# Hybrid decoder step: gates last in the input projection, weights split two products ahead, half of the first rotary keys gathered early

## The chip, the cores and the metric

One core of one Trainium2 chip runs the whole program in one launch. The metric is device microseconds of one execution, from its start to the end of the slowest (here the only) core. Engines are named as in the profile: PE (TensorE matmul), PEld (its weight load), DVE (VectorE), ACT (ScalarE), POOL (GpSimd), SP (the queue from which nearly all DMAs are issued).

## The reference, cut to what matters

Two layers of a decoder run on 1024 prompt tokens and 8 sample tokens together (1032 columns). In each layer the normalised input goes through one input projection whose columns feed three mixers:

```python
proj = h @ lp['w_in']
z, xbc, dt_raw, cq, ckv, kpe, u = jnp.split(proj, offs, axis=-1)
ssd_out, hT, conv_new = ssd_mixer(z, xbc, dt_raw, ...)   # conv width 4 + SiLU on xbc, scan, y * silu(z), norm
...                                                      # latent attention from cq, ckv, kpe
pool_out, pool_new = pool_mixer(u, pool_buf, pos, ...)   # trailing windows 2, 4, 8, 16
mix = jnp.concatenate([ssd_out, mla_out, pool_out], axis=-1) @ lp['w_out']
```

The gates z are needed only at the end of the SSD mixer (y times silu(z)); xbc after its convolution and SiLU is needed at its first chunk. The sample tokens attend over 8192 cached positions each, in pages; the rotary part of the cached keys is gathered by a page table.

## The kernel before

Activations lie transposed: 128 channels on the partitions, 1032 tokens in the free dimension. The input projection is 16 products of 128 output channels. In storage order they are: 0 the latent, 1 dt and the rotary key, 2 and 3 the query latent, 4 and 5 the pooling input u, 6 to 12 the convolved channels (6 to 8 x, 9 and 10 B, 11 and 12 C), 13 to 15 the gates z. The order in which they are computed is ORD.

A product is split in three in precision (a high and a low half of weights and of input, three matmuls for each of 8 contraction blocks) and in three thirds of tokens, so it is 72 matmuls of up to 348 columns. PSUM has four "d" banks and three "g" banks; a product takes two d and one g, so PE can be one product ahead of the evacuation.

For each product the weights take one DMA (`load_w`, line 123, tile wr), a cast of the high half on ACT (line 88, tile wh) and a subtraction for the low half on POOL (line 89, tile wl). `in_proj` loads and splits the weights of the next product before the gemm of this one. Then `evac` multiplies by the norm on DVE (line 285) and adds the bias on ACT (line 290). Products 6 to 12 are convolved on DVE (`conv`, lines 358 to 369: one long scale and three long multiply-adds, and four short ones for the sample tokens), which needs a second buffer, and two small stores per product go out on SP (lines 350 and 372), after the evacuation. Products 13 to 15 get their SiLU in `evac`, on ACT, followed by one of 8 columns for the sample tokens.

Beside the products, from index 8 on, `build` advances a side chain by one piece per product: `mla_prep` (index 8), `smp_prep` (9), `softplus` (10), `pool` (11 to 15). They are long on DVE and short on PE. The pooling piece loads spb, and the store o_spool (line 392) waits for it.

All of this shares one set of 24 buffers of 1032 columns ("a": weights, raw weights, projections, convolutions, temporaries) and one of 20 wider buffers ("b"). The 18 b buffers that hold the split input are released as the last product reads them; mv (the keys' map) takes the 19th, and the page tiles (pg), split pages (lt) and gathered rotary keys (kp) share what is left.

After the loop `conv_silu` runs SiLU over products 6 to 12 on ACT, with a function table loaded before and after, and the weave starts: `sample` (pages of all 8 sample tokens), the SSD chain and later the attention, interleaved by yields. `sample` asks for four pages, then issues 16 gathers from POOL (line 1094), eight to a kp tile, then splits the first page: high half on ACT (line 1141), low half on POOL (line 1142). `smp_kpe` multiplies the gathered keys in four blocks of four gathers each (line 1105). The SSD chain starts with decay masks (line 511 on PE, exponentials on ACT), B times C (line 544), transposes (line 558) whose results ACT and DVE copy out (lines 560 and 562), and the masked product (line 574).

Every engine takes its queue in order. The order in a queue follows the place in the program, but an instruction whose operands and buffer are there may be placed ahead of earlier ones that lack theirs; the table loads and the SiLUs of `conv_silu` are kept behind all ACT work written before them.

Of the kernel before, what the change touches and what calls it, by code (L numbers as in the profile page):

```python
# [48 lines left out]
class Net:  # L49
# [228 lines left out]
    def evac(self, o, ps, r, func=None):  # L278

        nc = self.nc  # L280
        n = T - 2 * TH
        b = self.S([128, 9], "sb", bufs=3)
        for t in range(3):
            a = slice(TH * t, min(TH * t + TH, T))
            nc.vector.tensor_tensor(out=o[:, a], in0=ps[t][:, :a.stop - a.start], in1=r[:, a], op=ALU.mult)
        nc.vector.tensor_copy(b, ps[2][:, n:n + 9])
        nc.vector.tensor_tensor(out=o[:, TP:], in0=o[:, TP:], in1=b[:, 1:9], op=ALU.add)
        if func is None:
            return b
        nc.scalar.activation(out=o[:, :TP], in_=o[:, :TP], func=func, bias=b[:, 0:1])  # L290
        if func == AF.Silu:
            nc.scalar.activation(out=o[:, TP:], in_=o[:, TP:], func=func)

    def sums(self, parts, mix=False):

# [8 lines left out]
    def in_proj(self, l, X, r):  # L304
        nc, A = self.nc, self.A
        out = self.pj = {}
        raws = {} if l else {2: self.w2}
        W = {}

        def prefetch(m):  # L310
            if m < 16 and m not in raws:
                raws[m] = self.load_w(A["win"][l, ORD[m]], 1024)

        def conv(m):
            if m < 16:
                W[m] = self.split_w(raws.pop(m), 1024)
        W[0] = self.w0
        pss = {}

        def wk(i):  # L320
            return lambda k: tuple(w[:, 128 * k:128 * k + 128] for w in W[i])
        if l == 0:

            W[1] = self.w1
            for i in range(2):
                pss[i] = self.psum3(TH)
            for ks in (range(0, 4), range(4, 8)):
                for i in range(2):
                    self.gemm(pss[i], wk(i), X, ks)
        for i, m in enumerate(ORD):  # L330
            if l or i:
                prefetch(i + 1)
                prefetch(i + WPI)
                conv(i + 1)
            if i in pss:
                ps = pss.pop(i)
            else:
                ps = self.psum3(TH)
                self.gemm(ps, wk(i), X)
            del W[i]  # L340
            t = self.C(name=f"pj{m}")
            self.evac(t, ps, r, AF.Silu if m >= 13 else AF.Identity)
            out[m] = t
            if 6 <= m < 13:
                out[m] = self.conv(l, m - 6, t)
            yield
# [26 lines left out]
        return y  # L373

    def conv_silu(self):
        for m in range(6, 13):
            y = self.pj[m]
            self.tc.keep_in_program_order(self.nc.scalar.activation(out=y, in_=y, func=AF.Silu))

# [873 lines left out]
    def sample(self, l):  # L1253
        self.held = False
        nc = self.nc
        n = NB * 4
        pages, kp, lts = {}, {}, []
        kts = {b: [] for b in range(NB + 1)}

        def want(t):  # L1260
            if t < 4 * n:
                pages[t] = self.fetch(l, t // 16, t % 16)

        def cut(t):
            if t < 4 * n:
                lts.append(self.smp_split(pages[t]))
        for i in range(FA):
            want(i)
        for i in range(16):
            self.smp_gather(l, 0, i, kts[0])  # L1270
        self.weave.spawn(self.smp_kpe(0, kts[0], kp), W_0)
        for i in range(SA):
            cut(i)
        yield W_9
        for gi in range(n):
            b, g = divmod(gi, 4)
            if g == 0:
                o = 390 * (b % 2)
                h = self.mv[:, o:o + 6]
                nc.vector.tensor_copy(h, self.qabs[:, b, :])  # L1280
                nc.vector.tensor_tensor(out=self.mv[:, 396 + o:402 + o], in0=self.qabs[:, b, :], in1=h.bitcast(F32),
                                        op=ALU.subtract)
                if b % 2 == 0:
                    og2 = self.B(name="og")[:, 0:1032].rearrange("p (b a x) -> p b a x", b=2, a=4)
                og = og2[:, b % 2]
            ss, sc = self.S([128, GP, 6], "ss", bufs=2), self.S([128, GP, 6], "scr", bufs=2)
            late = []
            for k in range(GP):
                t, c = divmod(GP * gi + k, 4)
                if c == 0:  # L1290
                    want(t + FA)
                    cut(t + SA)
                    lt = lts.pop(0)
                if b + 1 < NB:
                    e = GP * g + k
                    if e >= GS and (e - GS) % GE == 0 and (e - GS) // GE < 16:
                        self.smp_gather(l, b + 1, (e - GS) // GE, kts[b + 1])
                    if e == min(KE, 63):
                        self.weave.spawn(self.smp_kpe(b + 1, kts[b + 1], kp), max(0, KE - 63))
                if k % 2 == 0:  # L1300
                    sq = self.C(name="sqk")[:, 0:768].rearrange("p (a x) -> p a x", a=2)
                self.smp_page(b, lt, 128 * c, sq[:, k % 2, :], sc[:, k, :])
                if k % 2:
                    if len(late) == LD:
                        o, x = late.pop(0)
                        nc.vector.tensor_reduce(out=o, in_=x, axis=AX.X, op=ALU.add)  # L1306
                        del x
                    late.append((ss[:, k - 1:k + 1, :], sq.rearrange("p a (h e) -> p a h e", h=6)))
                    del sq
                yield  # L1310
            self.weave.spawn(self.smp_soft(l, gi, late, ss, sc, kp, og, pages))
# [396 lines left out]
def build(nc, tc, A):  # L1708
    with tc.tile_pool(name="c", bufs=1) as cp, tc.tile_pool(name="s", bufs=1) as sm, \
# [54 lines left out]
        for l in range(L):  # L1764
            mod = mods[l]
            if l:
                n.ahead(A["win"][l, ORD[0]])
            mid = [lambda i=i: n.ada(0, mod, i) for i in range(2)] if l == 0 else ()
            X, r = n.norm(l, xs, mod, 0, 1, V_GN1, mid)
            if l:  # L1770
                for k in range(8):
                    nc.sync.dma_start(A["xmid"][k], xs[k])
            del xs
            n.sconv = n.S([128, 7, 3, NB], "sconv", bufs=1)
            nc.sync.dma_start(n.sconv, A["sconv"][l])
            pr = n.in_proj(l, X, r)
            side = seq(n.mla_prep(l), n.smp_prep(l), n.softplus(l), n.pool(l))
            for m in range(16):
                next(pr)
                if l == 0 and 4 + m < ADB[0][0][1]:  # L1780
                    n.ada(l, mod, 4 + m)
                if m == 6:
                    n.table()
                if m >= 8:
                    next(side, None)
            for _ in side:
                pass
            del X, r, pr
            n.conv_silu()
            n.table()  # L1790
            n.weave = Weave()
            n.wqk = {}
            n.weave.spawn(n.sample(l))
            n.weave.spawn(seq(n.ssd_prompt(l), n.ssd_sample(l), n.ssd_finish(l), n.mla_prompt(l)))
            n.weave.spawn(seq(*[n.ada_blocks(a, mods[a], range(b, c), W_C) for a, b, c in ADB[l]]), W_E)
            n.weave.run()
            n.weave = None
            side = [None]
            op = n.out_proj(l, mod, (lambda m: A["xT"][m]) if l == 0 else (lambda m: A["xmid"][m]), side)
            X = {}  # L1800
            next(op)
            n.pj = None
            gs = n.norm_gain(l, mod, 4, V_GN2)
            n.up_first(l)
            side[0] = n.norm_half(0, mod, gs, 3, X)
            next(op)
            for _ in side[0]:
                pass
            for j in range(WA0):
                n.up_conv(l, WAH + j)  # L1810
            side = n.norm_half(1, mod, gs, 3, X)
            for _ in range(SD1):
                next(side)

            def sink(m, x):
                if l == L - 1:
                    nc.sync.dma_start(A["o_y"][m], x)
            xs = n.ffn(l, X, mod, side, sink)
            del X
# [1 line left out]

NA, NBUF = 24, 20
HALF = (slice(0, 512), slice(512, 1024))
ORD = (0, 1, 2, 3, 13, 14, 15, 4, 5, 6, 7, 8, 9, 10, 11, 12)

HOOK = None
W_D, W_X, W_Y, W_H = 2, 1, 1, 3
# [6 lines left out]
WAH = 3  # L1834
WPT, WPL, XPT, XPL, GUP = (0, 1, 2, 3), (0, 2, 4, 6), (), (1, 5, 7), 0
NG0, SD0, SD1, SDN, WLD = 2, 10, 6, 1, 3
WPI, GS, W_9 = 1, 16, 14
DCA, CVA = (0,), ()
SDO = 2
LD = 1  # L1840
# [169 lines left out]
```

## Time and profile before

| | us |
|---|---|
| median of 3 runs | 3703.59 (3699.99 to 3705.51) |
| profiled execution, its own time | 3702.83 |
| span of that execution in the trace | 3701.1 |
| PE busy | 3457.9 (93%) |
| DVE, ACT, POOL busy | 2346.1, 1733.8, 1542.7 |
| input projection of layer 0, evacuations | 73 to 280 |
| input projection of layer 1, evacuations | 1893 to 2113 |

PE is busy nearly all the time, so time is to be had where PE stands still or runs at the lower of its two clocks. Each layer has one input projection, and the two look alike in the trace; times below are from layer 1 unless layer 0 is named. In a timeline row the first number is the start, the second the length, and the bracket at the end says how long the engine stood idle before it and what it waited for.

### The profile page before, as it was taken

The page shows a single profiled execution, that of the slowest core. Times are in us where ns is not written, and L with a number is a line of the kernel's source. Part 1 is how long each engine was busy: PE and PEld are TensorE (multiplying, and loading weights), DVE is VectorE, ACT ScalarE, POOL GpSimd, SP SyncE. Part 2 cuts the span into 40 slices and gives each one's busy share as a digit, 9 for nine tenths or more (in the row PEclk, how much of TensorE's full clock was granted, in tenths as well). Part 3 has the DMA queues.
Part 4 walks back from the last instruction along what each step waited for, and adds up shares of the span by engine and source line. Part 5 has one row for each costly group of instructions (what it writes and reads, how often), then busy time and mean ns, then how long its engine had stood idle before and what let it go on. Part 6 is the DMA issues. An engine that isn't in the chain of part 4 may idle for free. (4 is left out here: it accounts for less than half of the span.)

```text
span 3701.1 us, 66621 instructions
## 1 busy us (share of the span) xinstructions
PE 3457.9 (93%) x23740; PEld 3103.2 (84%) x23740; DVE 2346.1 (63%) x4308; ACT 1733.8 (47%) x4459; POOL 1542.7 (42%) x1173
## 2 busy tenths in 40 slices
PE   8988999898987999999999799999988979999999
PEld 5986767677887999999999666677777979999999
DVE  4377787778778655542344687777787685555333
ACT  4216576677844333331132265677776443333220
POOL 1125454444244555542221355444452445555431
PEclk9989899999988999999999999999999989999999
DMA  5124555544443222242221346554443522121431
GB/s 197 49 57 139 167 178 159 177 144 115 141 137 98 84 83 75 80 171 88 80 81 44 84 132 185 183 147 120 117 117 117 160 83 87 70 86 69 176 99 69
DMA packets 255322, 430.10 MB, mean 116 GB/s; under 512 B 38736, under 2 KB 180944, under 8 KB 254992
## 3 DMA queue, kind: packets, MB, share of 16 engines
q1 hardware_dynamic: 246800, 409.04, 35.1%
q0 software_dynamic: 8192, 16.79, 1.8%
q8 instruction: 190, 3.11, 0.4%
q14 instruction: 140, 1.15, 0.1%
HBM read 372.84 MB, written 52.87 MB: 115 GB/s over the span
## 5 line engine op out<-in xcount | busy, mean ns | idle before, releaser
L1159 ACT ACTIVATE sqk<-psd 128x384 f32<-128x384 f32 x1024 | 496.8, 503 | 226.2 <-PE psd L135 172.7
L1142 POOL TENSOR_TENSOR lt<-pg,lt 128x512 fp32r<-128x512 f32 x256 | 310.1, 1220 | 537.7 <-ACT lt L1141 438.4
L1306 DVE TENSOR_REDUCE ss<-sqk 128x12 f32<-128x768 f32 x448 | 421.8, 945 | 131.0 <-ACT sqk L1159 129.7
L133 PE MATMUL psd<-mv,lt 128*128 128x390 f32 x1024 | 435.8, 427 | 3.3 <-ACT scr L1160 3.3
L134 PE MATMUL psd<-X,wp 128*128 128x258 f32 x1408 | 400.5, 284 | 3.2 <-DVE wp L89 3.2
L135 PE MATMUL psd<-X,wp 128*128 128x258 f32 x1408 | 400.8, 285 | 0.0
L133 PE MATMUL psd<-X,wp 128*128 128x258 f32 x1408 | 400.6, 284 | 0.0
L134 PE MATMUL psd<-mv,lt 128*128 128x390 f32 x1024 | 366.5, 358 | 6.2 <-POOL lt L1142 6.2
L135 PE MATMUL psd<-mv,lt 128*128 128x390 f32 x1024 | 366.0, 357 | 0.0
L134 PE MATMUL psg<-X,wp 128*128 128x258 f32 x1056 | 303.3, 287 | 35.5 <-DVE wp L89 35.5
L1094 POOL DMA_INDIRECT kp<-kpeT,kidx x256 | 251.7, 983 | 122.2 <-issue 93.3
L135 PE MATMUL psg<-X,wp 128*128 128x258 f32 x1056 | 302.6, 287 | 0.0
L133 PE MATMUL psg<-X,wp 128*128 128x258 f32 x1056 | 301.8, 286 | 0.0
L89 POOL TENSOR_TENSOR wl<-wr,wh 128x1024 fp32r<-128x1024 f32 x47 | 116.5, 2480 | 433.8 <-ACT wh L88 376.6
L133 PEld LDWEIGHTS psd<-mv,lt 128*128 128x128 f32 x1024 | 202.0, 197 | 97.5 <-issue 47.9
L133 PE MATMUL psd<-op,wh 128*128 128x348 f32 (+1 forms) x792 | 255.9, 325 | 18.8 <-ACT wh L88 15.9
L134 PE MATMUL psd<-op,wl 128*128 128x348 f32 (+1 forms) x792 | 254.9, 322 | 19.4 <-POOL wl L89 12.5
L134 PEld LDWEIGHTS psd<-X,wp 128*128 128x128 f32 x1408 | 268.6, 191 | 3.5 <-DVE wp L89 3.5
L133 PEld LDWEIGHTS psd<-X,wp 128*128 128x128 f32 x1408 | 269.3, 191 | 0.0
L135 PEld LDWEIGHTS psd<-X,wp 128*128 128x128 f32 x1408 | 268.9, 191 | 0.0
L135 PE MATMUL psd<-op,wh 128*128 128x348 f32 (+1 forms) x792 | 253.2, 321 | 1.8 <-POOL op L89 1.4
L89 POOL TENSOR_TENSOR wp<-wr,wp 128x512 fp32r<-128x512 f32 x128 | 166.9, 1304 | 197.9 <-ACT wp L88 195.6
(467 smaller groups left out, 9928.1 us busy)
## 6 DMA issues: line engine op xcount, KB each, us to landing
pg<-pages SPq DMA_DIRECT2D x1024, 129.0 KB
wa<-wada SPq DMA_DIRECT2D x96, 512.0 KB
wr<-wff SPq DMA_DIRECT2D x96, 512.0 KB
ar<-actd SPq DMA_DIRECT2D x44, 516.0 KB
actd<-G SPq DMA_DIRECT2D x40, 516.0 KB
wd<-wdn SPq DMA_DIRECT2D x48, 384.0 KB
wr<-win SPq DMA_DIRECT2D x32, 512.0 KB
wr<-wout SPq DMA_DIRECT2D x32, 512.0 KB
```

The costliest lines, as they stand in the source:

```text
L89: (eng or nc.gpsimd).tensor_tensor(out=l, in0=x, in1=h.bitcast(F32), op=ALU.subtract)
L133: nc.tensor.matmul(ps, wh, xh, start=start, stop=False)
L134: nc.tensor.matmul(ps, wl, xh, start=False, stop=False)
L135: nc.tensor.matmul(ps, wh, xl, start=False, stop=stop)
L1094: self.nc.gpsimd.indirect_dma_start(out=kts[-1][:, 128 * g:128 * g + 128], out_offset=None, in_=self.A["kpeT"], in_offset=bass.IndirectOff ...
L1142: nc.gpsimd.tensor_tensor(out=ll, in0=v, in1=lh.bitcast(F32), op=ALU.subtract)
L1159: nc.scalar.activation(out=sq, in_=d[:, kc], func=AF.Square)
L1306: nc.vector.tensor_reduce(out=o, in_=x, axis=AX.X, op=ALU.add)
```

## The change

The gates move to the end of the order and lose their SiLU in `evac`; `conv_silu` now runs it for all ten, in a new order. The mid-loop table load (index 6) goes. Weights are loaded three products ahead and split two ahead. The 16 gathers of the first sample token are written behind the twelfth product instead of at the start of `sample`.

```diff
 def evac(...):
         nc.scalar.activation(out=o[:, :TP], in_=o[:, :TP], func=func, bias=b[:, 0:1])
-        if func == AF.Silu:
-            nc.scalar.activation(out=o[:, TP:], in_=o[:, TP:], func=func)
 def in_proj(...):
         def prefetch(m):
-            if m < 16 and m not in raws:
+            if m < 16 and m not in raws and m not in W:
                 raws[m] = self.load_w(A["win"][l, ORD[m]], 1024)
         def conv(m):
-            if m < 16:
+            if m < 16 and m not in W:
                 W[m] = self.split_w(raws.pop(m), 1024)
...
             if l or i:
-                prefetch(i + 1)
-                prefetch(i + WPI)
-                conv(i + 1)
+                for j in range(1, WSA + 1):
+                    prefetch(i + j)
+                    conv(i + j)
+                prefetch(i + WSA + 1)
...
-            self.evac(t, ps, r, AF.Silu if m >= 13 else AF.Identity)
+            self.evac(t, ps, r, AF.Identity)
 def conv_silu(self):
-        for m in range(6, 13):
+        for m in (9, 11, 6, 7, 8, 10, 12, 13, 14, 15):
 def sample(...):
+        kts[0] = self.kt0
+        self.kt0 = None
...
-        for i in range(16):
-            self.smp_gather(l, 0, i, kts[0])
 def build(...):   # the loop over m in range(16)
-                if m == 6:
-                    n.table()
                 if m >= 8:
                     next(side, None)
+                if m == 11:
+                    n.kt0 = []
+                    for i in range(16):
+                        n.smp_gather(l, 0, i, n.kt0)
-ORD = (0, 1, 2, 3, 13, 14, 15, 4, 5, 6, 7, 8, 9, 10, 11, 12)
+ORD = tuple(range(16))
-WPI, GS, W_9 = 1, 16, 14
+WSA, GS, W_9 = 2, 16, 14
```

## Rows read from the trace of the kernel before

**Rows 1.** The page: span, and the granted clock in 40 slices.

```profile
span 3701.1 us, 66621 instructions
...
PEclk9989899999988999999999999999999989999999
```

**Rows 2.** Stretches of layer 1: length, busy of PE, PEld, DVE, ACT, POOL, clock, DMA.

```profile
1898.00:1985.00 87.00, 87.00 (x546) 86.70 (x545) 13.73 (x39) 17.61 (x19) 17.13 (x8) 1.00 0.08 25
...
2054.00:2066.00 12.00, 5.87 (x36) 5.58 (x35) 11.72 (x26) 2.20 (x2) 0.28 (x1) 0.88 0.39 76
2066.00:2073.00 7.00, 5.75 (x20) 5.30 (x20) 6.82 (x13) 1.15 (x1) 2.08 (x1) 0.50 0.45 20
```

**Rows 3.** PE's waits, 1860 to 2250 us: total us, times, longest.

```profile
PE psm L1105 <- DMA kp<-kpeT,kidx: 7.2, 2, 5.4
PE psd L134 <- POOL wl L89: 6.6, 5, 2.0
PE psd L133 <- ACT wh L88: 6.1, 1, 6.1
```

**Rows 4.** The same for layer 0, 60 to 400 us.

```profile
PE psd L133 <- ACT wh L88: 6.0, 1, 6.0
PE psm L1105 <- DMA kp<-kpeT,kidx: 5.5, 2, 3.8
PE psd L134 <- POOL wl L89: 4.3, 3, 1.6
```

**Rows 5.** SP's queue about the load of the fourteenth product's weights, timeline.

```profile
2056.16 0.42 SPq L387 DMA_DIRECT2D spb<-wpool  x1
2060.30 0.34 SPq L392 DMA_DIRECT2D o_spool<-spb  x1
2061.05 0.33 SPq L123 DMA_DIRECT2D wr<-win  x1
```

**Rows 6.** ACT, timeline: two weight casts, then the end of the projection.

```profile
2064.54 1.04 ACT L88 CAST wh<-wr 128x1024 fp32r<-128x1024 f32 x1 [9.26 <-DMA wr<-win]
...
2077.20 1.05 ACT L88 CAST wh<-wr 128x1024 fp32r<-128x1024 f32 x1 [9.69 <-DVE cv L362]
...
2112.51 1.15 ACT L290 ACTIVATE pj<-pj,sb 128x1024 f32<-128x1024 f32 x1
2113.68 1.28 ACT L378 ACT_TABLE_LOAD   x1
2114.98 6.78 ACT L378 ACTIVATE cv<-cv 128x1032 f32<-128x1032 f32 x7
2121.78 1.28 ACT L207 ACT_TABLE_LOAD   x1
...
2132.93 0.37 ACT L560 COPY xn<-psg 128x256 f32<-128x256 f32 x1 [8.05 <-PE psg L558]
```

**Rows 7.** POOL, timeline: a low weight half, the gathers (first, tenth, last), the pages.

```profile
2081.80 2.34 POOL L89 TENSOR_TENSOR wl<-wr,wh 128x1024 fp32r<-128x1024 f32 x1 [13.72 <-PE psg L135]
...
2103.40 1.36 POOL L1094 DMA_INDIRECT kp<-kpeT,kidx  x1 [7.00 <-PE psd L135]
...
2115.05 1.75 POOL L1094 DMA_INDIRECT kp<-kpeT,kidx  x1 [0.30 <-issue]
...
2123.74 0.94 POOL L1094 DMA_INDIRECT kp<-kpeT,kidx  x1 [0.30 <-issue]
2124.71 2.32 POOL L1142 TENSOR_TENSOR lt<-pg,lt 128x512 fp32r<-128x512 f32 x2
```

**Rows 8.** DVE's groups, 1985 to 2118 us: the convolutions' long multiply-adds.

```profile
L362 DVE SCALAR_TENSOR_TENSOR cv<-pj,vt,cv 128x1021 f32<-128x1021 f32 (+2 forms) x21 | 26.9, 1279 | 0.2
```

**Rows 9.** PE, timeline: the decay masks behind the last product, the first masked product.

```profile
2111.59 1.50 PE L511 MATMUL psg<-acr,kt 128*128 128x128 f32 x12
...
2134.76 0.88 PE L574 MATMUL psg<-M,xn 128*64 128x128 f32 x12 [0.46 <-DVE xn L562]
```

**Rows 10.** The 26 us behind the last product of layer 1, columns as in rows 2.

```profile
2111.60:2137.60 26.00, 17.06 (x74) 9.42 (x73) 12.58 (x31) 16.74 (x30) 14.67 (x14) 0.80 0.42 95
```

## The prediction

> **What bounds the kernel now.** I read the page first: a span of 3701.1 us, and a granted clock that stays at 9 tenths or more but for a few slices [rows 1]; with PE busy 93% of the span, a change pays only where PE stands still or is clocked down. So the second view was the table of stretches over one input projection, the third PE's list of waits there, and only then the timelines of the engines named in those waits. The reader is to see three places. The first seven products or so run without a gap: 87.00 us busy in 87.00, at full clock, 546 matmuls, which makes 0.159 us for one and 11.5 us for a product of 72 [rows 2]. The switches of ACT's tables for the gates lie in that stretch, so they cost nothing. Later, PE is busy only 5.87 of 12 us, and the 7 us behind that are granted 0.50, the lower of the two levels (1.2 GHz) [rows 2]. At the end, in the 26 us behind the last product, PE is busy 17.06 us at a mean grant of 0.80 [rows 10].
>
> The causes are in the lists of waits. One wait of 6.1 us (6.0 in layer 0) is for the high half of weights; several together of 6.6 us (4.3) for low halves; 7.2 us (5.5) for gathered keys [rows 3, 4]. The long one is a matter of SP's queue: the load of the fourteenth product's weights leaves at 2061.05, behind a store of the pooling state that must first see its own load land (issued from 2056.16, store at 2060.30) [rows 5]; the cast follows at 2064.54 after 9.26 us of waiting for that load [rows 6]. The last one is POOL's: 16 gathers from 2103.40 to 2124.7, released by the last product's reads of its input, and behind them the low halves of the first pages [rows 7].
>
> **The change, part by part.**
>
> *Weights ahead.* A load is now written three products ahead and a split two ahead, so in SP's queue the fourteenth load stands before the stores of the tenth product and before all of the pooling piece. A lead of two products is 23 us, against the 9.26 us for which the cast was late. I take the whole wait as gone: 6.1 + 6.0 = 12.1 us. What it leaves behind goes too: in the 7 us at the lower clock 20 matmuls took 5.75 us where they need 20 x 0.159 = 3.2 us, so 2.6 us a layer [rows 2], 5.2 in all (for layer 0 I use layer 1's row). Together 17.3 us; the bounds are 0 (the load is late for want of a buffer instead) and 17.3. The low halves' 6.6 + 4.3 = 10.9 us have another cause in part: one of them began only when the product before ended and freed its buffer (13.72 us behind PE) and one cast waited 9.69 us for a convolution to free one [rows 6, 7]. Being two ahead takes two or three more of the 24 a buffers, so it cures lateness and worsens the shortage. I take half, 5.4 us; bounds 10.9 and a loss that is rival 1.
>
> *Gates last, for DVE and buffers.* The number of finished projections at each index stays the same. But convolutions now fall on indices 6 to 12 instead of 9 to 15. On the stretch with the side chain (8 to 12) there are five where there were four, and DVE is already busy 11.72 of 12 us where it is worst [rows 2]. One more costs at least three long multiply-adds, 26.9 / 7 = 3.8 us [rows 8]. In exchange indices 13 to 15 have none, so DVE has only evacuations there, a convolution's second buffer is not asked for, and no small stores stand before the weights on SP. PSUM lets PE run one product ahead of DVE, which hides part of the crowding; without that cover it is 3.8 us a layer. Nearest to a middle, I charge half: 3.8 us in both layers; bounds 0 and 7.6.
>
> *ACT.* Two table loads (1.28 us each [rows 6]) and three short activations a layer go from the middle, where PE never waited: 0. Three SiLUs come to the end: the seven there took 6.78 us, 0.97 each, so 2.9 us more before the second table load and the masks' exponentials [rows 6].
>
> *Gathers.* The count of b buffers decides: 18 of 20 hold the split input, mv takes one, so one is free before the last product. The first kp tile gets it, and its eight gathers (0.94 us and a gap of 0.30 each, about 10 us of POOL [rows 7]) run beside the products, where POOL has gaps of over 13 us [rows 7]. The second kp tile must wait, as all sixteen did, for the last product's first third to free a buffer. It is the first in line then, where three pages stood ahead of kp before; a third of a product, 3.8 us, frees six tiles one by one, so I estimate its start at some 2 us before 2103.40. Eight gathers are 10 us, so POOL is free by about 2111.5 instead of 2124.7, at the end of the last product, and the pages' low halves follow at once. The first page loses its early buffer, and its load now stands with the others; if it lands late, the pages wait and the end gains less (rival 3).
>
> *The end of the stage.* With the gathers out of the way, the SSD chain is next. Before, ACT had done its SiLUs, table and exponentials by 2132.93 - 8.05 = 2124.9 and then stood idle 8.05 us for PE's transposes, which were queued behind the gathered keys and the pages [rows 6]. Now ACT gets there 2.9 us later, at 2127.8. So at most 8.05 - 2.9 = 5.1 us of the wait can be won, and the first masked product, at 2134.76 before and 23.2 us behind the last product [rows 9], comes at about 18 us. I take that for each layer: 10.2 us. Bounds: a loss of 2.9 us a layer if ACT's chain and not the gathers was the limit, and above, all of the 26 - 17.06 = 8.9 us that PE stood idle [rows 10].
>
> *Sum:* 17.3 + 5.4 - 3.8 + 10.2 = 29.1 us. The profiled execution took 3702.83 us (its span 3701.1), 0.8 below the median of the runs, so 3673.7, or 3674.5 as a median. I say 3675.
>
> **The rivals.**
>
> *1. Too few a buffers (slower).* Six or seven of the 24 hold weights while the side chain wants most of the rest. Then each low half starts only when the product before it ends, as the row at 2081.80 does once: a cast of 1.04 and a subtraction of 2.34 us, 3.4 us of PE standing still per product [rows 6, 7]. For n products a layer that is 6.8 n us, less the 10.9 us of today's waits. It outweighs the other three terms (17.3 - 3.8 + 10.2 = 23.7) from n = (23.7 + 10.9) / 6.8, that is from more than five products; at six (the tenth to the fifteenth) the time is 3703 + 6 = 3709. For it: both buffer waits quoted above. Against it: today's order has the same number of projections alive and shows such a wait clearly once a layer. Chance 0.13.
>
> *2. DVE becomes the bound of the projection.* The evacuations come late in 8 to 13, PE's one product of lead is used up, and the weights' gain is spent there; the whole of the 7.6 us and half of the 17.3 go. Time: 3703 + 7.6 - 8.6 - 10.2 = 3692. For it: DVE at 11.72 of 12 [rows 2]. Against: behind it DVE has three light products to catch up. Chance 0.15.
>
> *3. The end does not move.* The second kp tile is not first in line, or ACT's longer chain is the limit; the end gives between 0 and a loss of 5.8. Time: 3703 - 18.9 + (0 to 5.8), about 3687. Against: ACT's 8.05 us of idle [rows 6]. Chance 0.14.
>
> *4. The early gathers are slowed by DVE.* One gather took 1.75 us where another took 0.94 [rows 7]. If all eight do, they hold POOL 8 x 2.05 = 16.4 us; that exceeds a product's 11.5 us by 5 us, and a low half behind them could be that late once a layer. Time: 3674 + 10 = 3684. Against: splits are two products ahead. Chance 0.03. The Trainium skill's page "SBUF — State Buffer" (section "SBUF: two separate sides", the "DVE blocks DMA" trap) speaks against this part of the change: a DMA issued from GpSimd's queue has its descriptors written by GpSimd, which VectorE locks out of the shared port while it runs certain instructions. By that, gathers moved among convolutions are the wrong ones to move; the row of 1.75 us agrees in kind, and by its size it would stay hidden.
>
> **How the numbers follow.** My forecast has 0.55. All but rival 1 end faster; within rival 2 I allow a third to end near no change. A measurement of this kernel tells about 0.2%, 7.4 us, from no change. Faster: 0.55 + 0.14 + 0.03 + 0.10 of rival 2, less 0.06 for what re-ordered queues may do further on: 0.76. Within: the 0.05 left of rival 2, and 0.05 of that 0.06: 0.10. Slower: rival 1 and the 0.01 left: 0.14. The forecast's own bounds: all upper bounds, 17.3 + 10.9 + 17.8, give 3657, and full clock at the end a few us more; with no cure for the low halves, the full crowding and half of the end (17.3 - 7.6 + 5.1), 3688. For 8 in 10 I take in rivals 2 to 4 and the edge of no change: 3654 to 3705.
>
> **What would show it.** Right: the list of waits without the wait for wh of some 6 us, and no stretch at 0.50 behind it; the load of the fourteenth product's weights on SP before the pooling store; eight gathers before the last product and eight in it; POOL's first page split within 2 us of the last product's end; ten SiLUs and the masked product about 18 us behind the last product. The time from the seventh product to the end of the last should shrink by about 9 us a layer. Wrong: new waits of PE on wl behind a cast that waited for PE or DVE (rival 1), evacuations that PE waits for (rival 2), kp still waited for (rival 3).

## The result, and the profile after

The changed kernel takes 3663.51 us (median of 4 runs, 3663.32 to 3671.33) against 3701.79 (3696.68 to 3705.51) on the same chip: ratio 0.9899, 95% interval 0.9884 to 0.9913. It is faster by some 38 us, where 28 were forecast; the time lies inside the range. The profiled execution took 3663.35 us. Its page, beside [rows 1]:

```profile
span 3661.6 us, 66619 instructions
...
PEclk9999799999998999999999998999999989999999
```

To see where the time came from, I cut both traces at the same events. In DVE's timeline every product ends with a copy into sb. Two pairs of such rows mark, in layer 1, the end of the ninth product (index 8) and of the last; first the kernel before, then the one after:

```profile
1984.76 0.16 DVE L286 COPY sb<-psg 128x9 f32<-128x9 f32 x1
...
2112.21 0.16 DVE L286 COPY sb<-psg 128x9 f32<-128x9 f32 x1
```

```profile
1964.31 0.16 DVE L286 COPY sb<-psg 128x9 f32<-128x9 f32 x1
...
2081.72 0.16 DVE L286 COPY sb<-psg 128x9 f32<-128x9 f32 x1
```

Call this stretch P (the last seven products): 127.5 us before, 117.4 after. The first masked product follows at 2134.76 [rows 9], and in the kernel after:

```profile
2081.09 1.50 PE L510 MATMUL psg<-acr,kt 128*128 128x128 f32 x12
...
2099.22 1.12 PE L573 MATMUL psg<-M,xn 128*64 128x128 f32 x12
```

Call the stretch from the last copy up to it E: 22.5 and 17.5 us. The spans, 3701.1 and 3661.6, differ by 39.5 us:

| | layer 0 | layer 1 |
|---|---|---|
| start of the program to the end of index 8 | 0.9 | |
| P (126.8, 127.5 before) | 11.7 | 10.0 |
| E (22.8, 22.5 before) | 5.2 | 5.0 |
| first masked product of layer 0 to the first product of layer 1 | | -1.0 |
| first product to the end of index 8 | | 3.6 |
| first masked product of layer 1 to the end | | 3.9 |

So 32 of 39.5 us are in the two stretches that the prediction spoke of. The stretch between them, from the first masked product of layer 0 to layer 1, varies from 1584 to 1598 us over all the profiles of this study, and the one behind them from 1560 to 1576. The five shortest of the former all belong to kernels with the new order, but three others with that order, this one among them, took 1593 to 1594 us; the latter follows no edit. So neither of these two rows is put down to the change.

The table of stretches splits P into PE's own work and its standing still (columns as in rows 2). Before, then after, layer 1:

```profile
1984.80:2112.30 127.50, 112.34 (x635) 104.08 (x634) 88.24 (x177) 30.63 (x41) 22.04 (x14) 0.89 0.30 71
```

```profile
1964.40:2081.80 117.40, 106.72 (x637) 96.98 (x636) 81.01 (x168) 31.00 (x42) 32.60 (x23) 0.96 0.28 74
...
2081.70:2107.70 26.00, 18.68 (x105) 12.95 (x106) 12.29 (x32) 24.00 (x49) 6.92 (x8) 0.87 0.39 107
```

PE stood still for 127.50 - 112.34 = 15.2 us before and 10.7 after. The same 635 or so matmuls took 5.6 us less, at a mean granted clock of 0.96 instead of 0.89. By these two profiles over half of this layer's gain in P is clock, not waiting. (Layer 0: 14.9 us of standing still became 7.7, and 111.9 us of work became 107.5.) That split is not firm. An experiment below leaves the gates' SiLU out behind the loop; in P its PE, DVE, ACT and POOL run the same instructions in the same order as here, and its row for layer 1 is:

```profile
1966.90:2084.70 117.80, 110.57 (x638) 100.45 (x637) 81.04 (x169) 30.77 (x42) 32.06 (x23) 0.93 0.29 74
```

P is as long (117.7 us), but with 7.2 us of standing still at a clock of 0.93; in layer 0 it is 118.0 us, where this kernel has 115.2. So from one profile to the next P repeats to some 3 us, and what it is made of less well.

The second row of the kernel after (from 2081.70) answers to [rows 10]: in the 26 us behind the last product PE is busy for 18.68 us instead of 17.06.

PE's list of waits, layer 1 (1830 to 2220 us) and layer 0 (60 to 370 us), against [rows 3, 4]:

```profile
PE psd L133 <- DVE pb L419: 5.7, 1, 5.7
PE psg L510 <- ACT M L518: 3.6, 1, 3.6
...
PE psg L134 <- POOL wl L89: 2.8, 1, 2.8
PE psd L134 <- POOL wl L89: 2.0, 1, 2.0
...
PE psm L1104 <- DMA kp<-kpeT,kidx: 0.4, 1, 0.4
```

```profile
PE psd L133 <- DVE pb L419: 3.8, 1, 3.8
...
PE psg L134 <- POOL wl L89: 2.8, 1, 2.8
```

The wait for wh is gone, and that for gathered keys falls from 7.2 us to 0.4. In their place stands one for DVE (line 419 is a short pooling operation placed among the evacuation's three multiplies of line 285; what PE needs is a PSUM bank that they free) and one for ACT's exponentials at the end. Where the first comes from is seen in the timelines of PE, DVE and POOL:

```profile
2057.86 0.32 PE L135 MATMUL psg<-op,wh 128*128 128x348 f32 x1
...
2064.43 0.63 PE L133 MATMUL psd<-op,wh 128*128 128x348 f32 x1 [5.67 <-DVE pb L419]
2064.85 0.49 PE L134 MATMUL psd<-op,wl 128*128 128x348 f32 x1
```

```profile
2043.07 1.25 DVE L409 SCALAR_TENSOR_TENSOR pj<-pb,kt,pj 128x1008 f32<-128x1008 f32 x1
2044.25 2.34 DVE L411 TENSOR_TENSOR pb<-pb,kt 128x16 f32<-128x16 f32 x1
...
2059.98 3.19 DVE L409 SCALAR_TENSOR_TENSOR pj<-pb,kt,pj 128x1008 f32<-128x1008 f32 x1
2063.09 0.16 DVE L411 TENSOR_TENSOR pb<-pb,kt 128x16 f32<-128x16 f32 x1
...
2063.77 0.51 DVE L285 TENSOR_TENSOR pj<-psd,r 128x348 f32<-128x348 f32 x1
```

```profile
1983.78 0.96 POOL L1093 DMA_INDIRECT kp<-kpeT,kidx  x1
...
1987.55 1.30 POOL L1093 DMA_INDIRECT kp<-kpeT,kidx  x1 [0.31 <-issue]
...
2012.92 2.38 POOL L89 TENSOR_TENSOR wl<-wr,wh 128x1024 fp32r<-128x1024 f32 x1 [2.15 <-ACT wh L88]
2042.08 4.48 POOL L89 TENSOR_TENSOR wl<-wr,wh 128x1024 fp32r<-128x1024 f32 x1 [26.78 <-DVE pb L403]
2059.22 2.88 POOL L89 TENSOR_TENSOR wl<-wr,wh 128x1024 fp32r<-128x1024 f32 x1 [12.66 <-ACT wh L88]
...
2070.86 0.96 POOL L1093 DMA_INDIRECT kp<-kpeT,kidx  x1 [8.75 <-PE psd L134]
...
2079.62 0.95 POOL L1093 DMA_INDIRECT kp<-kpeT,kidx  x1 [0.31 <-issue]
2080.59 1.20 POOL L1141 TENSOR_TENSOR lt<-pg,lt 128x512 fp32r<-128x512 f32 x1
```

PE had run as far ahead of DVE as its PSUM banks allow and then stood 5.67 us, until DVE came to the evacuations at 2063.77. DVE had spent 3.19 us on a pooling operation that took 1.25 us at 2043.07. The 3.19 us overlap POOL's subtraction from 2059.22 to 2062.10. The matmuls behind this wait take 0.49 us instead of 0.32, so it goes with a lower clock as well. The gathers come as forecast in number, eight early and eight in the last product. But the early ones start at 1983.78, within the product of index 9: they were placed ahead of work written before them.

SP's queue (against [rows 5]) and the end of the projection on ACT (against [rows 6]):

```profile
2019.92 0.34 SPq L123 DMA_DIRECT2D wr<-win  x1
2036.25 0.34 SPq L384 DMA_DIRECT2D spb<-spool  x1
2040.79 0.82 SPq L391 DMA_DIRECT2D o_spool<-spb  x2
```

```profile
2082.02 1.15 ACT L290 ACTIVATE pj<-pj,sb 128x1024 f32<-128x1024 f32 x1
2083.19 1.28 ACT L377 ACT_TABLE_LOAD   x1
2084.48 6.78 ACT L377 ACTIVATE cv<-cv 128x1032 f32<-128x1032 f32 x7
2091.17 2.95 ACT L377 ACTIVATE pj<-pj 128x1032 f32<-128x1032 f32 x3
2094.13 1.28 ACT L207 ACT_TABLE_LOAD   x1
...
2097.11 0.38 ACT L559 COPY xn<-psg 128x256 f32<-128x256 f32 x1
```

Even the fifteenth product's load, the first of these rows, stands before the pooling piece; the fourteenth's left earlier still. At the end ACT now works without a pause from its last bias (2082.02) to the copy at 2097.11; the idle 8.05 us that stood before this copy are gone. The end is ACT's chain: 15.1 of 17.5 us.

### The profile page after: what moved, and what is told of

Read it like the earlier page. It is cut to its first block, busy times and chain, and to the rows that moved or that the text cites. A ratio compares the mean times of both kernels' runs of the same rounds, so it can differ in the third digit from the quotient of the medians.

```text
span 3661.6 us, 66619 instructions
## 1 busy us (share of the span) xinstructions
PE 3436.4 (94%) x23740; PEld 3091.1 (84%) x23740; DVE 2358.1 (64%) x4308; ACT 1732.6 (47%) x4455; POOL 1546.8 (42%) x1173
## 5 line engine op out<-in xcount | busy, mean ns | idle before, releaser
L89 POOL TENSOR_TENSOR wl<-wr,wh 128x1024 fp32r<-128x1024 f32 x47 | 125.7, 2679 | 374.5 <-ACT wh L88 288.3
L133 PE MATMUL psd<-op,wh 128*128 128x348 f32 (+1 forms) x792 | 252.6, 319 | 18.1 <-DVE pb L419 9.5
L134 PE MATMUL psd<-op,wl 128*128 128x348 f32 (+1 forms) x792 | 251.0, 317 | 10.5 <-DVE wl L89 5.7
```

The lines of the kernel that those rows point to most:

```text
L89: (eng or nc.gpsimd).tensor_tensor(out=l, in0=x, in1=h.bitcast(F32), op=ALU.subtract)
L133: nc.tensor.matmul(ps, wh, xh, start=start, stop=False)
L134: nc.tensor.matmul(ps, wl, xh, start=False, stop=False)
```

## The experiments

Three parts were put into the kernel before one by one, taken out of the one after one by one, and two of them varied: **G** (gathers early), **W** (weights split two ahead), **O** (gates last, SiLU of the gates at the end, no table load in the loop). All stages come from one profiled execution, medians and ratios (to the kernel before on the same chip) from all runs. The experiments ran on three further chips, on which the kernel before has medians of 3705.01, 3707.95 and 3709.97 us, so the ratios and not the medians are to be compared from row to row.

| kernel | median, us | ratio, 95% interval | P, layers 0 / 1 | E, layers 0 / 1 | layer 1's P: PE busy, idle, clock |
|---|---|---|---|---|---|
| before | 3701.79 | | 126.8 / 127.5 | 22.8 / 22.5 | 112.3, 15.2, 0.89 |
| after (G, W, O) | 3663.51 | 0.9899 (0.9884 to 0.9913) | 115.2 / 117.4 | 17.5 / 17.5 | 106.7, 10.7, 0.96 |
| G alone | 3702.29 | 0.9991 (0.9982 to 1.0) | 132.9 / 130.0 | 14.7 / 14.7 | 114.0, 16.0, 0.91 |
| W alone | 3692.30 | 0.9959 (0.9945 to 0.9973) | 116.7 / 117.0 | 22.5 / 23.2 | 108.9, 8.1, 0.93 |
| O alone | 3693.61 | 0.997 (0.9956 to 0.9984) | 132.9 / 133.0 | 20.6 / 20.8 | 114.4, 18.7, 0.86 |
| after without G | 3674.86 | 0.9918 (0.9906 to 0.9931) | 118.5 / 120.8 | 21.3 / 21.1 | 111.1, 9.7, 0.92 |
| after without O | 3672.76 | 0.9908 (0.9889 to 0.9927) | 119.2 / 117.8 | 14.7 / 14.7 | 109.3, 8.4, 0.93 |
| after without W | 3713.81 | 1.0015 (1.0004 to 1.0027) | 141.9 / 141.6 | 17.5 / 17.5 | 118.7, 22.9, 0.84 |

**The gathers alone** (into the kernel before):

```diff
+        kts[0] = self.kt0
-        for i in range(16):
-            self.smp_gather(l, 0, i, kts[0])
...
+                if m == 11:
+                    n.kt0 = []
+                    for i in range(16):
+                        n.smp_gather(l, 0, i, n.kt0)
```

> The kernel before with the early gathers alone. My theory: the end of the stage is a term of its own, about 5 us a layer, so 3702 - 10 = 3692, and PE's wait for kp is gone while its wait of 6 us for wh stays. Perhaps a little more than 5 us, because ACT has seven SiLUs there and not ten: up to 8 us a layer, 3686. Rival: the gathers help only once the convolution of the last product is gone from the end too; then within 4 us of before.

E falls by 8 us a layer, to 14.7, yet the whole is unchanged within 0.2%: P is longer by 6.1 and 2.5 us, and the 7 us that the two stages still gain do not reach the end. The first half of the keys' product now lies inside P, while the waits for weights are still there. PE's timeline of layer 0 and its waits in layer 1:

```profile
197.17 1.92 PE L1105 MATMUL psm<-kp,bd 128*32 128x512 f32 x2 [0.25 <-DVE mall L1061]
199.89 1.74 PE L1105 MATMUL psm<-kp,bd 128*32 128x512 f32 x2
```

```profile
PE psd L133 <- ACT wh L88: 6.6, 2, 5.4
PE psd L134 <- POOL wl L89: 6.6, 4, 2.0
```

**The weights alone:**

```diff
-                prefetch(i + 1)
-                prefetch(i + WPI)
-                conv(i + 1)
+                for j in range(1, WSA + 1):
+                    prefetch(i + j)
+                    conv(i + j)
+                prefetch(i + WSA + 1)
```

> The kernel before with the weights split two products ahead and nothing else. My theory: the two waits for weights and the slow clock behind them are what the projection lost, and the lead alone takes them away: 17.3 + 5.4 us, so about 3679; the waits for gathered keys stay. Rival: without the gates at the end, buffers or DVE take the place of the weights, and nothing or a loss remains: 3698 to 3710.

P falls by 10.2 and 10.5 us and E nearly stays: this part and no other carries P. The ratio makes 15 us of the 20 that the two stages gain, and 26 had been expected. The waits for weights are gone from PE's list over P, but it now has one for DVE in each layer, before the last product, though the order is the old one (layer 1):

```profile
PE psd L133 <- DVE pj L285: 4.2, 1, 4.2
```

**The order alone:**

```diff
-            self.evac(t, ps, r, AF.Silu if m >= 13 else AF.Identity)
+            self.evac(t, ps, r, AF.Identity)
...
-        for m in range(6, 13):
+        for m in (9, 11, 6, 7, 8, 10, 12, 13, 14, 15):
...
-ORD = (0, 1, 2, 3, 13, 14, 15, 4, 5, 6, 7, 8, 9, 10, 11, 12)
+ORD = tuple(range(16))
```

> The kernel before with the gates last and their SiLU in the final pass, weights one ahead, gathers at the start of the sample stage. My theory: one more convolution beside the side chain costs up to 4 us in both layers together, and the three SiLUs hide behind the gathers, so 3702 to 3706, and PE's wait of 6 us for wh stays. Rival: the order itself brings the projection's gain, because indices 13 to 15 have no convolution: 3680 to 3690.

P grows by 6.1 and 5.6 us, E shrinks by 2.1 and 1.7, so the two stages lose 8 us; the median of nine runs nevertheless fell by 0.3%. Beside W it is the same: from W alone to after without G the stages lose 2 us, and yet the ratio falls from 0.9959 to 0.9918, with intervals apart. So what the order gives lies outside P and E. Part of it can be seen just behind E: the last masked product of layer 1, before and here, the first one being at 2134.76 and 2134.37:

```profile
2228.33 0.44 PE L574 MATMUL psg<-M,xn 128*64 128x128 f32 x4
```

```profile
2219.69 0.44 PE L572 MATMUL psg<-M,xn 128*64 128x128 f32 x4
```

The masked products take 85.3 us instead of 93.6 (layer 0: 85.5 instead of 93.0), and beside W 85.7 instead of 92.5. In the kernel after they take 85.1, but there the time is lost again before layer 1 starts (the row of -1.0 above). The profiled execution of the order alone was the slowest of its nine (3704.71), so how much of this reaches the end, and why, stays open.

**After without the gathers:**

```diff
-        kts[0] = self.kt0
...
+        for i in range(16):
+            self.smp_gather(l, 0, i, kts[0])
...
-                    for i in range(16):
-                        n.smp_gather(l, 0, i, n.kt0)
```

> The changed kernel with the gathers put back to the start of the sample stage. My theory: terms add up, so it loses the end's 10 us against the changed kernel: about 3674, with PE waiting 5 to 7 us a layer for kp again. Rival (the early gathers slow the projection by holding GpSimd): it loses less than 5 us.

Beside W and O the gathers are worth 3.8 and 3.6 us of E and 3.3 and 3.4 of P, 14 us in all by the stages, though P repeats only to some 3 us; by the ratios they are worth 0.2%, with intervals that overlap.

**After without the new order:**

```diff
+        if func == AF.Silu:
+            nc.scalar.activation(out=o[:, TP:], in_=o[:, TP:], func=func)
...
-ORD = tuple(range(16))
+ORD = (0, 1, 2, 3, 13, 14, 15, 4, 5, 6, 7, 8, 9, 10, 11, 12)
```

> The changed kernel with the old order (gates at indices 4 to 6, their SiLU in the evacuation): gathers and weights alone. From the four runs so far: weights alone bring the projection's last seven products to 116.8 us a layer and gathers alone the end to 14.6. My theory now: those two carry the whole change and the order is worth nothing by itself: 116.8 + 14.6 and some 2.5 us of key products that move into the projection, 134 us a layer as in the changed kernel (132.7 and 134.9), so 3660 to 3668. Rival: the order makes room for the early gathers, and without it the projection is 3 to 6 us a layer longer, as it was with gathers alone: 3670 to 3676.

Nearly all of the gain is there without the order: P is 4.0 and 0.4 us longer than after, E is 2.8 shorter in each layer. The two intervals overlap, so beside G and W the order is not shown to be worth anything.

**After without the weights ahead:**

```diff
-                for j in range(1, WSA + 1):
-                    prefetch(i + j)
-                    conv(i + j)
-                prefetch(i + WSA + 1)
+                prefetch(i + 1)
+                prefetch(i + WPI)
+                conv(i + 1)
...
-WSA, GS, W_9 = 2, 16, 14
+WPI, GS, W_9 = 1, 16, 14
```

> The changed kernel with the weights one ahead as before (order and gathers alone). My theory: the wait of 6 us for wh is back in both layers, with the slow clock behind it and the low halves' waits; the order alone made the two stretches 4 us a layer longer, the gathers 2 to 5 shorter: within 6 us of before, 3696 to 3708. Rival: gates last shorten the queue in front of the weights, so most of the gain stays: 3675 to 3690.

P is 142 us, the longest of all, at a clock of 0.84 in layer 1. The wait for wh is back (layer 1, one of PE's rows):

```profile
PE psd L133 <- ACT wh L88: 8.4, 2, 6.6
```

**Loads ahead, splits not** (the kernel before; this tests the reason that I gave for the late cast, SP's queue):

```diff
-WPI, GS, W_9 = 1, 16, 14
+WPI, GS, W_9 = 3, 16, 14
```

> The kernel before with the weights loaded three products ahead and split one ahead as before. My theory: the wait of 6 us for wh is lateness in SP's queue, so the load's place alone takes it away with the slow clock behind it, and the last seven products go from 127 to about 118 us a layer, near the 117 of weights alone; about 3690. Rival: the split's lead, not the load's, is what counts (the cast and the subtraction behind convolutions and missing buffers): 124 to 127 us a layer, no measurable change.

Median 3699.72, ratio 0.9972 (0.9957 to 0.9987); P 130.5 and 125.1 us. The profiled execution (3716.99) was the slowest of ten, so it does not show where the 0.3% of the ratio come from. The wait for wh shrinks to 2.2 us, but the low half takes its place. PE's waits, then ACT and POOL, layer 1:

```profile
PE psd L134 <- POOL wl L89: 11.1, 4, 6.3
...
PE psd L133 <- ACT wh L88: 2.2, 2, 1.2
```

```profile
2064.90 1.04 ACT L88 CAST wh<-wr 128x1024 fp32r<-128x1024 f32 x1 [3.02 <-PE psg L135]
```

```profile
2068.50 4.48 POOL L89 TENSOR_TENSOR wl<-wr,wh 128x1024 fp32r<-128x1024 f32 x1 [27.52 <-issue]
```

The cast now waits for the end of an earlier product on PE, not for its load; the row of the low half names nothing that it waited for. So an early load was not enough: the split must be ahead as well. That the split's lead works through getting its buffers before the pooling's temporaries ask for them fits these rows, but was not tried by itself.

**The gates' SiLU left out** (after; what part of the end ACT's three new SiLUs make):

```diff
-        for m in (9, 11, 6, 7, 8, 10, 12, 13, 14, 15):
+        for m in (9, 11, 6, 7, 8, 10, 12):
```

> The changed kernel without the SiLU of the gates (left out altogether, three of 0.98 us a layer at the end). My theory: ACT's chain is what sets the end now, so the first masked product comes 2.9 us a layer earlier, 17.5 to 14.6 us behind the last product's evacuation: about 3657. Rival: PE's own work at the end or the transposes are the limit: no difference.

E is 14.6 us in both layers, so three SiLUs cost 2.9 us of E, as long as their row on ACT (2.95). In all three kernels with G and seven SiLUs at the end E is 14.6 to 14.7 us, and in all three with G and ten it is 17.5 (the third of these has the side chain earlier, below). The whole, 3672.94 us, ratio 0.9905 (0.9885 to 0.9925), did not move: P was 118.0 and 117.7, and what is left of the stages' gain, 2.6 us, is below what the medians can tell.

**SiLUs in the loop** (after; nine of ten written behind the fifteenth product, the last behind the sixteenth):

```diff
-    def conv_silu(self):
-        for m in (9, 11, 6, 7, 8, 10, 12, 13, 14, 15):
+    def conv_silu(self, ms):
+        for m in ms:
...
+                if m == 14:
+                    n.conv_silu((9, 11, 6, 7, 8, 10, 12, 13, 14))
+                if m == 15:
+                    n.conv_silu((15,))
```

> The changed kernel with nine of the ten SiLUs written behind the fifteenth product, into the 7 us in which ACT waits for the last one. My theory: with ACT's chain cut from ten SiLUs to one, PE's own 8 us of work and two or three short steps set the end: the first masked product 11 us behind the last evacuation, 6 us a layer less, about 3651. Rival: the nine SiLUs (8.7 us) delay the last product's evacuation or the table is loaded once more, and the gain is under 2 us a layer: 3659 to 3664.

3653.51 us, ratio 0.9862 (0.9839 to 0.9884); E 8.2 and 7.9 us, P 118.0 and 118.1. On ACT the SiLUs now run during the last product:

```profile
2067.98 1.28 ACT L377 ACT_TABLE_LOAD   x1
2069.28 6.79 ACT L377 ACTIVATE cv<-cv 128x1032 f32<-128x1032 f32 x7
...
2078.96 1.15 ACT L290 ACTIVATE pj<-pj,sb 128x1024 f32<-128x1024 f32 x1
```

This is shown: ACT's chain sets the end. By the program it is the gates' place at the end of the order that lets nine SiLUs start so early, since all convolutions are done by then; this edit was not tried with the old order.

**The side chain four products earlier** (after):

```diff
-                if m >= 8:
+                if m >= 4:
```

> The changed kernel with the side chain started at index 4 instead of 8 (its operands are complete at index 3, and indices 4 and 5 have no convolution). My theory: what is left in the projection, some 12 us a layer over 80 us of products and 24 of side matmuls, is DVE's crowding by convolutions beside the side chain; spread out, the twelve products from index 3 lose 6 to 10 us a layer, about 3647. Rival: PE's waits inside the side chain's own small steps and the slow clock behind them are the loss and only move: 3660 to 3666.

3655.42 us, ratio 0.9857 (0.9839 to 0.9875). From the end of index 3 to the end of the last product: 170.6 and 168.2 us, where after has 172.5 and 174.8 (and 175.3 and 175.1 in the profile without the gates' SiLU). So there was more to be won beside the side chain, and PE's wait for DVE before the last product is gone; the stages' 8.5 us do not hold the whole difference of the ratios.

**Both together:** the two edits above (shown in part).

```diff
-                if m >= 8:
+                if m >= 4:
                     next(side, None)
+                if m == 14:
+                    n.conv_silu((9, 11, 6, 7, 8, 10, 12, 13, 14))
+                if m == 15:
+                    n.conv_silu((15,))
```

> The last two edits together: nine SiLUs written behind the fifteenth product, the side chain from index 4. My theory: one acts on the end and one on the projection, so the gains add: about 9 us a layer at the end and what the side chain's move gives, 3636 to 3645. Rival: with the projection compressed, ACT's nine SiLUs no longer fit before the last product: no better than the better of the two.

3647.69 us, ratio 0.983 (0.9811 to 0.9848), E 7.6 us in both layers: better than both kernels, and the best of the study, though its interval just touches that of the side chain's move alone.

## Why the prediction came out as it did

**Weights ahead: right in place, and in size as far as P tells.** The wait of 6.1 and 6.0 us for wh is gone, and W alone shortens P by 20.6 us where 17.3 + 5.4 = 22.7 were summed. For all parts together 17.3 + 5.4 - 3.8 = 18.9 us of P were summed; the trace after has 21.7, the one without the gates' SiLU, with the same work in P, 18.6.

The single terms were not met as well. The slow clock was put at 5.2 us for both layers, from the 20 matmuls in the 7 us behind the wait. But the 7 us were not the only ones; a stretch ahead of them, in the products of index 10 and 11, had run at 0.59:

```profile
2015.00:2036.00 21.00, 19.49 (x107) 18.48 (x107) 12.46 (x35) 3.54 (x8) 3.24 (x2) 0.59 0.20 45
```

Over all of P, PE's own work became shorter by 4.4 us in layer 0 (111.94 to 107.50) and 5.6 in layer 1, 10.1 in all, and its standing still fell by 7.2 and 4.5 us, 11.6, where 12.1 + 5.4 - 3.8 = 13.7 were summed. Without the gates' SiLU the same two numbers are 5.5 and 12.9, close to what was summed, so one profile does not settle how P's gain divides between clock and waits. For low halves 5.4 us were summed; their waits fell from 10.9 [rows 3, 4] to 2.8 + 2.0 + 2.8 = 7.6, by 3.3. One reading was loose: the 9.26 us are the time that ACT stood idle before the cast, and what the late cast cost PE is the 6.1.

**Its reason: half right.** I put the late cast down to SP's queue. Loading ahead alone took most of the wait for wh away and gave it to the low half. What the prediction said of low halves, that buffers and not loads make them late, fits the cast of that run, which waited for PE; for its low half the profile names no cause.

**DVE's crowding: in another place, and little of it the order's.** Charged 3.8 us, bounds 0 and 7.6. The waits for DVE are 3.8 and 5.7 us and come at the last product, not at indices 8 to 12, where I placed them: PE's lead had covered the crowding until then. But W alone, in the old order, has waits of 4.2 us there in each layer, and without the gates' SiLU, with the same work in P, they are 5.7 and 1.1. So this wait is what stands next once the weights are early, and no more than a small part of the 9.5 us is shown to be the order's. By P the order's price depends on the rest: alone it adds 11.6 us, beside W 1.8 + 3.8 = 5.7, and beside W and G it takes 4.4 away. What makes the last figure negative was not found; it is little more than P varies by itself.

**Gathers: right in count, wrong in place.** The second eight start 10.9 us before the last evacuation (2081.72 - 2070.86), where all sixteen started 8.8 us before it (2112.21 - 2103.40): the 2 us earlier that were estimated. The first page's low half begins at 2080.59, ahead of the last evacuation. I had not seen that the gathers would start two products before their place in the program, nor that the first half of the keys' product would follow them into P, where it costs when waits are still there (G alone) and nothing visible when they are not.

**The end: right.** About 18 us were forecast, counted from the masks behind the last matmul; so counted, 2099.22 - 2081.09 = 18.1 were measured, and for both layers 10.3 us of E where 10.2 were forecast. It was limited by ACT, as reasoned from the 8.05 us of idle time, and the SiLUs' 2.9 us were exact.

**Not forecast:** 3.7 us early in layer 1, where the second product ends 7.2 us behind the first instead of 10.9. It is 7.2 us in three of the kernels with W and 8.7 in five, 9.3 with G but without W, and 10.9 with neither, so weights and gathers both seem to bear on it; its cause is not settled. With 3.9 us behind the last masks, which no edit explains, this makes up most of the 10 us between forecast and trace; the rest is P's 2.8, which P varies by.

**The rivals.** 1 (too few a buffers) came only as a trace: two casts of layer 1 began when a product of PE had ended (2037.47 and 2058.10), but PE waited for neither's high half. The shortage shows once a layer, in the low half at 2042.08 that waited for a pooling temporary, and cost 2.8 us, of which 2.1 are the time that this subtraction ran longer than the one at 2012.92 (4.48 instead of 2.38 us). 2 (DVE the bound) came in small, as the waits for DVE above. 3 fell with E. 4 fell too: the slowest early gather took 1.30 us, and no low half was late for it.

## What to carry to other kernels

A wait of PE can cost clock besides its length. Read PE's busy time, its standing still and its granted clock over the whole stretch, not only at the few matmuls behind the wait, and take the split from more than one profile: here the same work got 0.93 and 0.96. The clock does not simply follow the standing still either: in P of layer 0, after without G stood still for 13.2 us at 0.96, after without O for 7.5 us at 0.90. Loading early helps only as far as the work on the load (here cast and subtraction) is early too, so trace the next step of the chain before putting a wait down to the queue where it is seen. When a stage's end is freed from one engine, look at once for the next engine's chain there: starting ACT's SiLUs within the last product won more of E (18.9 us over both layers) than the change did (10.3).

## What the hardware showed

DVE and POOL held each other up: the DVE operation of 128 x 16 elements at 2044.25 took 2.34 us, 0.16 at 2063.09, and ended with POOL's subtraction (2042.08 + 4.48 = 2046.56), which itself took 4.48 us instead of 2.38. The Trainium skill's page "SBUF — State Buffer", section "SBUF: two separate sides", describes such a lock: a VectorE operation with two inputs in SBUF and a GpSimd operation that reads SBUF exclude each other for the whole instruction. The trace agrees: the 3.19 us from 2059.98 are 2.12 us up to the end of POOL's subtraction and 1.07 behind it, near the 1.25 us of the operation undisturbed.
